# Hybrid diffusion step on one core: the last two column blocks of w_d go one token tile at a time, and three casts are issued sooner

## The chip, the core and the metric

The kernel runs on one core of one Trainium2 chip. The metric is the time of one execution on the device, in microseconds (us). Before the change three runs gave 1954.19, 1956.51 and 1957.05; the median is 1956.51. One further execution was profiled: it took 1956.43, and its span, from the first to the last instruction, is 1954.6. All views of the profile come from that one, and positions in it are given in us from the start of the span.

## The reference, cut to what matters

There are 384 tokens (128 of a context, 256 of a latent) of 2048 channels, in float32, and one layer. The change touches the dense SwiGLU feed-forward at the layer's end and the sums around it:

```python
h = rmsnorm(x, lw['norm_pre_ffn']) * (1.0 + sc2) + sh2
ff = (jax.nn.silu(h @ lw['w_ffn_gate']) * (h @ lw['w_ffn_up'])) @ lw['w_ffn_down']
x = x + ga2 * rmsnorm(ff, lw['norm_post_ffn'])
```

`w_ffn_gate` and `w_ffn_up` are 2048 x 5632, `w_ffn_down` is 5632 x 2048. The last line needs the whole of a token's row of `ff` before its root mean square is known. The output is the new `x`.

## The kernel before, in words

All products are made from float32 values cut into a high and a low part (`whi`, `wlo` for a weight, `hid_hi`, `hid_lo` for an activation); a product is three TensorE products, high by high, high by low, low by high. ScalarE casts the high part of each weight tile (L1430), VectorE subtracts for the low part (L1441), four of each are in store, and the two raw buffers are filled by DMAs that SyncE (SP) issues.

The 5632 hidden channels are worked through in 11 chunks of 512 (index `c`, `FC = 4` blocks of 128). For each chunk the gate and up products are made, the gated activation is turned so that hidden channels lie on partitions (`turn_hid`, L1596, into the PSUM tile `ptr`), cut into its two parts (L1598), and multiplied by the chunk's rows of `w_d` (`products`, L1532). The hand-written list `steps` sets the order of all of it; small pieces of work for ScalarE and VectorE are queued in the lists `now` and `pend`, and pieces of `pend` are taken out, three or so at a time, whenever the next weight is split (`split_next`, `settle_pend`). An engine runs its instructions in the order in which they were issued.

Partial sums of `ff` lie in twelve SBUF tiles `unit(t, n)` of 128 x 512, tile name `psums`: token tile `t` of 0 to 2, column block `n` of 0 to 3. The last chunk's activation, `hidE`, meets the eight last weights of `w_d`: for each column block, in the order 0, 2, 1, 3 (`d_order`), two weights of half a chunk each (`kh` 0 and 1). Every weight serves all three token tiles, 18 products; after a block's second weight `add_last` (L1676, L1677) adds the PSUM tile `pdn` to `unit(t, n)` and squares and sums it on ScalarE into `ssq`.

Behind the last product the root mean square of each token tile is formed in `r3` (`factor`, L1804 and L1805, and `inverse`, L1808). `scale` (L1813 on ScalarE, L1815 on VectorE) multiplies the units of token tiles 0 and 1, or, for tile 2, the identity `dg` (L1842). `turn(k, t)` turns a 128 x 128 piece into the PSUM tile `py[k]` (L1826, L1828), which holds all 384 tokens of 128 channels. Each `py[k]` is multiplied by the gate in `mods` and added to the residual `x1b`, by VectorE alone (L1862) or by ScalarE and GpSimd (L1855, L1856), and every second `k` a store of 384 KB goes to `out_yT` (L1867). Runs of 384 tokens of one channel are contiguous there.

`hid_sums` (L1606) forms sums of the activation for four products in place of more in the `w_d` part of chunks before the last; it is called from chunk 1 on a VectorE sum (`spare`, L1781), and from later chunks on the PSUM tiles.

Of the kernel before, what the change touches and what calls it, by code (L numbers as in the profile page):

```python
# [20 lines left out]
P = 128  # L21
# [75 lines left out]
def tile_step(ctx: ExitStack, tc: tile.TileContext, a, o):  # L97
# [947 lines left out]
    with ExitStack() as s:  # L1045
# [239 lines left out]
        def unit(t, n):  # L1285

            return psums[n // 2][:, 3 * (n % 2) + t, :]
# [310 lines left out]
            pend.extend([lambda: ACT.copy(hi, pt), lambda: DVE.tensor_sub(lo, pt, hi.bitcast(F32))])  # L1598
            return pt

        def hid_sums(h1, h2):

            r, (hi, lo) = dt["raw"], dt["S"]
            add, sub = DVE.tensor_add, DVE.tensor_sub
            return [
                lambda: ACT.copy(r[:, 3], h2[:, 0:2]),  # L1606
                lambda: add(r[:, 0], r[:, 3], h2[:, 2:4]), lambda: sub(r[:, 1], r[:, 0], h1[:, 0:2]),
                lambda: sub(r[:, 2], h1[:, 2:4], r[:, 1]), lambda: sub(r[:, 3], h1[:, 0:2], r[:, 3]),
                lambda: ACT.copy(hi, r),
            ]  # L1610
# [58 lines left out]

        ssq = pf.tile([P, 3, 4], F32, name="ssq")  # L1670
        r3 = pf.tile([P, 3], F32, name="r3")
        dg = ep[0][:, 0:P]

        def add_last(t, n, p, done):

# [11 lines left out]
        d_bank, hid_pt = {}, []  # L1687
        for kind, c, i in steps:
            last_c = c == NFC - 1 and kind == "D"
            if last_c and hid_last is not None and x1b is None:  # L1690
                while pend:
                    pend.pop(0)()
                x1b = actp.tile([P, KT, T], F32, tag="A_hi", name="x1b")
                for q in range(4):
                    SP.dma_start(x1b[:, 4 * q : 4 * q + 4, :], x1_d[:, 4 * q : 4 * q + 4, :])
                ACT.activation(tmp1, eps_t, AF.Sqrt)
            if kind == "D":
                w = grab2()
                n, kh = i // 2, i % 2
# [10 lines left out]
                    (pd_tiles[t], [[x[:, 2 * kh + m, t * P : (t + 1) * P] for m in range(2)] for x in h], mov_d, kh == 0, kh == 1)  # L1710
                    for t in ts
                ]
                products(w, todo, by_tile=last_c and kh == 1)
                if kh == 1:
                    if not last_c:
                        for t in range(3):
                            if c < LAST - 1:
                                pend.append(lambda k=10 + 3 * (n - 2) + t, p=pd_tiles[t], c=c: to_sums(k, p, c))
                            else:
                                pend.append(lambda u=unit(t, n), p=pd_tiles[t]: out(u, p))  # L1720
                    else:
                        if done < 3:
                            for t in range(3):
                                pend.append(lambda t=t, n=n, p=pd_tiles[t], d=done: add_last(t, n, p, d))
                        if done == 1:
                            pend.append(lambda: DVE.tensor_add(r3, ssq[:, :, 0], ssq[:, :, 1]))
                        if done == 2:
                            pend.append(lambda: DVE.tensor_add(r3, r3, ssq[:, :, 2]))
                        done += 1
                if (c, i) == (NFC - 2, 6):  # L1730

                    while pend:
                        pend.pop(0)()
                    hid_last = tuple(actp.tile([P, FC, T], F32R, tag=t, name="hidE") for t in ("C_hi", "C_lo"))
                    for t in range(3):
                        turn_hid(hid_last, t, psm, "mm")
            elif kind[0] == "D":
                w = grab2()
                while pend:
# [10 lines left out]
            else:  # L1750
# [19 lines left out]
                if kind == "A" and i:  # L1770
# [7 lines left out]
                    if c < LAST and i == 2:  # L1778
                        if c == 1:
                            f = dt["full"]  # L1780
                            pend.append(lambda: DVE.tensor_add(f, hid[0][:, :, P:T].bitcast(F32), hid[1][:, :, P:T].bitcast(F32)))  # L1781
# [19 lines left out]
        n = d_order[-1]  # L1801

        def factor(t):
            DVE.tensor_add(r3[:, t : t + 1], r3[:, t : t + 1], ssq[:, t, 3:4])  # L1804
            ACT.activation(r3[:, t : t + 1], r3[:, t : t + 1], AF.Sqrt, bias=eps_t[:, 0:1], scale=1.0 / D)  # L1805

        def inverse(t):
            DVE.reciprocal(r3[:, t : t + 1], r3[:, t : t + 1])  # L1808

        def scale(eng, t, n):  # L1810
            f = unit(t, n)
            if eng is ACT:
                ACT.mul(f, f, r3[:, t : t + 1])  # L1813
            else:
                eng.tensor_scalar_mul(f, f, r3[:, t : t + 1])  # L1815

        py = {}
        places = [(pss, "side")] * 5 + [(psm, "mm")] * 3

        def turn(k, t):  # L1820
            if k not in py:
                pool, tag = places[k % 8]
                py[k] = pool.tile([P, T], F32, tag=tag, name="py")
            dst, src = py[k][:, t * P : (t + 1) * P], unit(t, k // 4)[:, (k % 4) * P : (k % 4 + 1) * P]
            if t < 2:
                PE.transpose(dst, src, ident)  # L1826
            else:
                PE.matmul(dst, src, dg, start=True, stop=True)  # L1828

        add_last(0, n, pd_tiles[0], 3)  # L1830
        add_last(1, n, pd_tiles[1], 3)
        factor(0)
        factor(1)
        add_last(2, n, pd_tiles[2], 3)
        inverse(0)
        inverse(1)
        scale(DVE, 0, 0)
        scale(DVE, 1, 0)
        factor(2)
        scale(DVE, 0, 1)  # L1840
        inverse(2)
        DVE.tensor_scalar_mul(dg, ident, r3[:, 2:3])  # L1842
        scale(DVE, 1, 1)
        for k0, t in ((0, 0), (0, 1), (4, 0), (0, 2), (4, 1), (4, 2)):
            for k in range(k0, k0 + 4):
                turn(k, t)
        on_act = (1, 3, 5, 7, 9, 11)
        for k in range(KT):
            if k >= 8:
                for t in range(3):  # L1850
                    turn(k, t)
            if k in on_act:
                tmp = ep[1 + k // 2 % 5][:, 0:T]
                for lo, hi, cd in segs:
                    ACT.mul(tmp[:, lo:hi], py[k][:, lo:hi], mods[:, 5, k, cd : cd + 1])  # L1855
                POOL.tensor_add(x1b[:, k, :], x1b[:, k, :], tmp)  # L1856
                if k in (3, 7):
                    for t in range(2):
                        scale(ACT, t, 2 + k // 4)
            else:  # L1860
                for lo, hi, cd in segs:
                    DVE.scalar_tensor_tensor(  # L1862
                        x1b[:, k, lo:hi], py[k][:, lo:hi], mods[:, 5, k, cd : cd + 1], x1b[:, k, lo:hi],
                        op0=ALU.mult, op1=ALU.add,
                    )
            if k % 2:
                (ACT if k == KT - 1 else SP).dma_start(o["yT"][:, k - 1 : k + 1, :], x1b[:, k - 1 : k + 1, :])  # L1867


# [76 lines left out]
```

## Time and profile before

| what | value |
|---|---|
| median of three runs | 1956.51 us |
| the profiled execution's own time | 1956.43 us |
| its span | 1954.6 us |
| TensorE busy | 1935.7 us, 99% |
| VectorE busy | 1639.9 us, 84% |
| ScalarE busy | 1011.9 us, 52% |
| GpSimd busy | 144.4 us, 7% |
| last product of w_d issued | 1937.6 us |
| last addition to the residual ends | 1949.9 us |

A group in the profile is written as line, engine, operation, output tile <- input tiles, shape. PE is TensorE, DVE VectorE, ACT ScalarE, POOL GpSimd, SPq the queue of SyncE that issues DMAs. What stands in square brackets is how long the engine was idle just before and whose end released it. Modelled ends of TensorE products overlap, so two starts in a row say more than one duration.

### The profile page before, as it was taken

The page shows a single profiled execution, that of the slowest core. Times are in us where ns is not written, and L with a number is a line of the kernel's source. Part 1 is how long each engine was busy: PE and PEld are TensorE (multiplying, and loading weights), DVE is VectorE, ACT ScalarE, POOL GpSimd, SP SyncE. Part 2 cuts the span into 40 slices and gives each one's busy share as a digit, 9 for nine tenths or more (in the row PEclk, how much of TensorE's full clock was granted, in tenths as well). Part 3 has the DMA queues.
Part 4 walks back from the last instruction along what each step waited for, and adds up shares of the span by engine and source line. Part 5 has one row for each costly group of instructions (what it writes and reads, how often), then busy time and mean ns, then how long its engine had stood idle before and what let it go on. Part 6 is the DMA issues. An engine that isn't in the chain of part 4 may idle for free.

```text
span 1954.6 us, 28091 instructions
## 1 busy us (share of the span) xinstructions
PE 1935.7 (99%) x10522; PEld 1715.2 (88%) x10522; DVE 1639.9 (84%) x2047; ACT 1011.9 (52%) x1468; POOL 144.4 (7%) x172
## 2 busy tenths in 40 slices
PE   8999999999999999999999999999999999999998
PEld 6779999999999999999988888888888888888876
DVE  5569788878876797977799989999999999988975
ACT  4233454454335655446456555555556565656444
POOL 0000000000000000004000111111112021111001
PEclk9999999999999999999999999999999999999999
DMA  9977677767764687655447686786869595949463
GB/s 389 374 259 266 222 251 238 226 220 258 249 200 155 218 269 242 215 173 201 144 145 245 160 237 171 217 206 194 222 182 234 169 239 158 264 117 254 134 212 108
DMA packets 212456, 422.05 MB, mean 216 GB/s; under 512 B 16732, under 2 KB 115228, under 8 KB 207968
## 3 DMA queue, kind: packets, MB, share of 16 engines
q1 hardware_dynamic: 193744, 386.31, 58.8%
q0 software_dynamic: 18432, 33.56, 11.1%
q8 instruction: 82, 1.34, 0.3%
q14 instruction: 54, 0.44, 0.1%
q10 hardware_dynamic: 144, 0.39, 0.1%
HBM read 365.68 MB, written 54.53 MB: 215 GB/s over the span
## 4 chain that ended last, share of the span: by engine, by line
PE 94%; DMA 2%; DVE 2%; ACT 1%; issue 0%; SPq 0%; POOL 0%; DVEq 0%; ACTq 0%; POOLq 0%
PE pmm L258 35%; PE pgu L1532 30%; PE pdn L1532 10%; PE pds L1532 7%; PE pv L398 3%; PE pgm L381 1%; DMA slab<-in_w_ada 1%; PE pf L996 1%; PE px L416 1%; PE pmm L1251 1%; PE ptr L1596 1%; DMA raw<-in_w_d 1%; DVE wlo L1441 1%; PE po L645 1%; PE pf L997 0%
## 5 line engine op out<-in xcount | busy, mean ns | idle before, releaser
L258 PE MATMUL pmm<-A_hi,whi 128*128 128x384 f32 x1200 | 404.5, 337 | 0.0
L258 PE MATMUL pmm<-A_hi,wlo 128*128 128x384 f32 x1200 | 401.6, 335 | 0.0
L258 PE MATMUL pmm<-A_lo,whi 128*128 128x384 f32 x1200 | 401.5, 335 | 0.0
L1430 ACT CAST whi<-u 128x1024 fp32r<-128x1024 f32 x200 | 209.5, 1052 | 154.2 <-PE pgu L1532 49.9
L224 ACT CAST whi<-raw 128x1024 fp32r<-128x1024 f32 x181 | 190.0, 1052 | 187.7 <-DMA raw<-in_w_gate 65.7
L225 DVE TENSOR_TENSOR wlo<-raw,whi 128x1024 fp32r<-128x1024 f32 x179 | 218.4, 1222 | 57.0 <-ACT whi L224 56.2
L1430 ACT CAST whi<-raw 128x1024 fp32r<-128x1024 f32 x157 | 165.4, 1053 | 185.0 <-DMA raw<-in_w_d 49.4
L1441 DVE TENSOR_TENSOR wlo<-u,whi 128x1024 fp32r<-128x1024 f32 x200 | 242.6, 1220 | 17.3 <-ACT whi L1430 16.6
L1532 PE MATMUL pgu<-whi,A_hi 128*128 128x512 f32 x640 | 252.5, 394 | 1.4 <-ACT ep L1573 0.9
L1532 PE MATMUL pgu<-whi,A_lo 128*128 128x512 f32 x640 | 249.6, 390 | 0.0
L258 PEld LDWEIGHTS pmm<-A_hi,whi 128*128 128x128 f32 x1200 | 225.4, 188 | 2.9 <-issue 1.8
L258 PEld LDWEIGHTS pmm<-A_lo,whi 128*128 128x128 f32 x1200 | 225.4, 188 | 0.2
L258 PEld LDWEIGHTS pmm<-A_hi,wlo 128*128 128x128 f32 x1200 | 225.3, 188 | 0.0
L572 DVE SCALAR_TENSOR_TENSOR adacc<-adaw,spad,adacc 128x1024 f32<-128x1024 f32 x180 | 222.9, 1280 | 2.5 <-DMA adaw<-in_w_ada 2.3
L1441 DVE TENSOR_TENSOR wlo<-raw,whi 128x1024 fp32r<-128x1024 f32 x157 | 191.6, 1220 | 15.3 <-ACT whi L1430 12.9
L1532 PE MATMUL pgu<-wlo,A_hi 128*128 128x512 f32 x640 | 186.0, 390 | 0.0
L1532 PEld LDWEIGHTS pgu<-whi,A_hi 128*128 128x128 f32 x640 | 120.2, 188 | 28.9 <-ACT whi L1430 2.0
L1532 PEld LDWEIGHTS pgu<-wlo,A_hi 128*128 128x128 f32 x640 | 120.2, 188 | 25.5
L1532 PEld LDWEIGHTS pgu<-whi,A_lo 128*128 128x128 f32 x640 | 120.3, 188 | 24.2
L1532 PE MATMUL pgu<-whi,S 128*128 128x512 f32 x400 | 117.6, 392 | 0.0
L1642 POOL DMA_DIRECT2D sums_d<-dw x64 | 58.4, 948 | 642.5 <-ACT dw L1638 637.2
L1532 PE MATMUL pdn<-whi,hid_hi 128*128 128x512 f32 x264 | 102.8, 390 | 0.0
(401 smaller groups left out, 3273.0 us busy)
## 6 DMA issues: line engine op xcount, KB each, us to landing
adaw<-in_w_ada SPq DMA_DIRECT2D x96, 512.0 KB, 4.3
raw<-in_w_d SPq DMA_DIRECT2D x70, 512.0 KB, 3.7
slab<-in_w_ada SPq DMA_DIRECT2D x32, 1024.0 KB
raw<-in_w_gate SPq DMA_DIRECT2D x64, 512.0 KB, 4.5
raw<-in_w_g SPq DMA_DIRECT2D x48, 512.0 KB, 4.7
raw<-in_w_u SPq DMA_DIRECT2D x48, 512.0 KB, 6.3
raw<-in_w_in SPq DMA_DIRECT2D x44, 512.0 KB, 4.5
u<-in_w_u SPq DMA_DIRECT2D x40, 512.0 KB, 7.6
```

Source lines behind the costliest of these rows:

```text
L224: ACT.copy(hi, raw)
L225: sub = lambda: eng.tensor_sub(lo, raw, hi.bitcast(F32))
L258: PE.matmul(dst, w[wi][:, k * n + n0 : k * n + n0 + P], x[xi][:, k0 + k, :], start=first and k == 0 and j == 0, stop=last and k == kts - 1 ...
L381: PE.matmul(pgv[q : q + 32, :], spad[:, k, :], slab[k // (KT // 2)][:, k % (KT // 2), :], start=k < 4, stop=k >= KT - 4,)
L398: PE.matmul(pv[2 * t + g], hT[x_][:, kb, t * P : (t + 1) * P], w_[:, g * 512 : (g + 1) * 512], start=kb == 0 and j == 0, stop=kb == KT - 1 ...
L416: PE.matmul(px, w_[:, u * P : (u + 1) * P], hT[x_][:, kb, :], start=j == 0, stop=j == 2)
L572: DVE.scalar_tensor_tensor(acc[:, c, :], w, spad[:, k, c : c + 1], acc[:, c, :], op0=ALU.mult, op1=ALU.add,)
L645: PE.matmul(dst, w[wi], x[xi], start=first and j == 0, stop=last and j == 2)
L1430: ACT.copy(hi, src)
L1441: DVE.tensor_sub(lo, src, hi.bitcast(F32))
L1532: PE.matmul(dst, stat[x_][m], mov(w[w_], m), start=first and w_ == m == x_ == 0, stop=last and w_ == m == 1, skip_group_check=any(more),)
L1642: POOL.dma_start(sums_d[k], u, accum_op=ALU.add)
```

## The change

Four things are changed.

First, in `hid_sums` for chunk 1 the copy of L1606 is issued on VectorE and no longer on ScalarE.

Second, after the last activation is turned (`turn_hid` for `hidE`), its three casts and then its three low parts are issued at once; before they stayed in `pend` behind the next weight's cast.

Third, the last two column blocks (`n` 1 and 3, four weights) are no longer run weight by weight. The four weights are collected in `late_w`, and `block(t, g)` runs the six products of weight `g` for one token tile `t` only. So tile 0 goes through all four weights, then tile 1, then tile 2.

Fourth, the tail is by token tile. When tile `t` has its last sum, `factor` forms its root mean square and scales all its four units, two on VectorE and two on ScalarE. Its 16 pieces are turned in groups of four into one PSUM tile (`bk`, eight banks, planned by hand in `sums_at` and `turned_at`), between the blocks of the next tile. `residual` adds 128 x 128 pieces on VectorE, or multiplies four on ScalarE and adds them at once on GpSimd. `store` sends four channel blocks of one token tile: 256 KB, in runs of 512 bytes, twelve stores on SP in place of eight.

```diff
-        def hid_sums(h1, h2):
+        def hid_sums(h1, h2, copy=ACT.copy):
...
-                lambda: ACT.copy(r[:, 3], h2[:, 0:2]),
+                lambda: copy(r[:, 3], h2[:, 0:2]),
...
+            if last_c and done >= 2:
+                late_w.append(grab2())
+                if len(late_w) == 4:
+                    while pend:
+                        pend.pop(0)()
+                continue
...
-                products(w, todo, by_tile=last_c and kh == 1)
+                products(w, todo)
...
                     for t in range(3):
                         turn_hid(hid_last, t, psm, "mm")
+                    for x in (0, 2, 4, 1, 3, 5):
+                        pend[x]()
+                    pend.clear()
...
-                            pend.extend(hid_sums(f[:, :, 0:P], f[:, :, P:]))
+                            pend.extend(hid_sums(f[:, :, 0:P], f[:, :, P:], DVE.tensor_copy))
...
+        bk = [pss.tile([P, 512], F32, tag="side", name="bk") for _ in range(5)]
+        bk += [psm.tile([P, 512], F32, tag="mm", name="bk") for _ in range(3)]
+        sums_at = ((5, 3), (6, 4), (7, 0))
+        turned_at = ((1, 2, 5, 3), (6, 4, 1, 2), (5, 3, 7, 0))
+
+        def block(t, g, fill=()):
+            n, kh = d_order[2 + g // 2], g % 2
+            stat = [[x[:, 2 * kh + m, t * P : (t + 1) * P] for m in range(2)] for x in hid_last]
+            products(late_w[g], [(bk[sums_at[t][g // 2]], stat, mov_d, kh == 0, kh == 1)])
+            if kh:
+                add_last(t, n, bk[sums_at[t][g // 2]], 2 + g // 2)
+                if fill:
+                    turn(1, 1)
+                    for _ in range(2):
+                        fill.pop(0)()
+                r = r3[:, t : t + 1]
+                DVE.tensor_add(r, r, ssq[:, t, 2 + g // 2 : 3 + g // 2])
+
+        def factor(t, fill=()):
+            r = r3[:, t : t + 1]
+            if fill:
+                fill.pop(0)()
+            ACT.activation(r, r, AF.Sqrt, bias=eps_t[:, 0:1], scale=1.0 / D)
+            DVE.reciprocal(r, r)
+            for n in (0, 2, 1, 3):
+                f = unit(t, n)
+                if n < 2:
+                    DVE.tensor_scalar_mul(f, f, r)
+                else:
+                    ACT.mul(f, f, r)
+            if fill:
+                fill.pop(0)()
+
+        def turn(t, n):
+            for j in range(4):
+                dst, src = (x[:, j * P : (j + 1) * P] for x in (bk[turned_at[t][n]], unit(t, n)))
                 PE.transpose(dst, src, ident)
...
+        def residual(t, n, on_act=False, later=False):
+            p = bk[turned_at[t][n]].rearrange("p (j c) -> p j c", j=4)
+            x = x1b[:, 4 * n : 4 * n + 4, t * P : (t + 1) * P]
+            g = lambda j: mods[:, 5, 4 * n + j, min(t, 1) : min(t, 1) + 1]
+            tmp = ep[4 + n % 2].rearrange("p (j c) -> p j c", j=4)
+            def add(j):
+                DVE.scalar_tensor_tensor(x[:, j, :], p[:, j, :], g(j), x[:, j, :], op0=ALU.mult, op1=ALU.add)
+
+            if later:
+                return [lambda j=j: add(j) for j in range(4)]
+            for j in range(4):
+                if on_act:
+                    ACT.mul(tmp[:, j, :], p[:, j, :], g(j))
+                else:
+                    add(j)
+            if on_act:
+                POOL.tensor_add(x, x, tmp)
+
+        def store(t, n):
+            SP.dma_start(o["yT"][:, 4 * n : 4 * n + 4, t * P : (t + 1) * P], x1b[:, 4 * n : 4 * n + 4, t * P : (t + 1) * P])
+
+        for g in range(4):
+            block(0, g)
         factor(0)
...
+        for t in (1, 2):
+            block(t, 0)
+            block(t, 1)
+            turn(t - 1, 0)
+            turn(t - 1, 2)
+            block(t, 2)
+            if t == 1:
+                turn(0, 1)
+            turn(t - 1, 3)
+            residual(t - 1, 0)
+            residual(t - 1, 2, True)
+            if t == 1:
+                residual(0, 1)
+            residual(t - 1, 3, True)
+            fill = []
+            if t == 2:
+                fill = residual(1, 1, later=True)
+            block(t, 3, fill)
+            factor(t, fill)
+            for n in (0, 2, 3, 1):
+                store(t - 1, n)
+        for n in (0, 2, 1, 3):
+            turn(2, n)
+            residual(2, n, n == 2)
+        for n in (0, 1, 2, 3):
+            store(2, n)
```

On VectorE, at the sums of chunk 1 (`dw` is the tile of the sums, `spare` the whole activation, `u` and `raw` weights):

```order
 L1413 TENSOR_TENSOR u_9223<-u_9221,u_9223 128x1024
 L1441 TENSOR_TENSOR wlo<-u_9222,whi 128x1024
-L1781 TENSOR_TENSOR spare<-hid_hi,hid_lo 128x1024
+L1786 TENSOR_TENSOR spare<-hid_hi,hid_lo 128x1024
+L1606 COPY dw<-spare 128x256
 L1607 TENSOR_TENSOR dw<-dw,spare 128x256
 L1441 TENSOR_TENSOR wlo<-raw,whi 128x1024
```

The copy now stands between the sum it reads and the addition that reads it, on the same engine; on ScalarE it stood ahead of two evictions of L1573.

On ScalarE, at the last activation and the last weights of `w_d`:

```order
-L1430 CAST whi<-raw 128x1024 x6
+L1430 CAST whi<-raw 128x1024 x5
 L1598 CAST hidE<-ptr 128x4x128 x3
-L1696 ACT_TABLE_LOAD
-L1696 ACTIVATE tmp_88<-eps_t 128x1
+L1430 CAST whi<-raw 128x1024
+L1695 ACT_TABLE_LOAD
+L1695 ACTIVATE tmp_88<-eps_t 128x1
 L1430 CAST whi<-raw 128x1024 x3
```

The three casts of `hidE` moved ahead of one weight cast.

On TensorE, the end of the program before (`py` the turned output, `ep_7617` the scaled identity):

```order
-L1532 MATMUL pdn<-whi,hidE 128x512 x4
-L1532 MATMUL pdn<-wlo,hidE 128x512 x2
-L1826 MATMUL py<-ident,psums 128x128 x12
-L1828 MATMUL py<-ep_7617,psums 128x128 x4
-L1826 MATMUL py<-ident,psums 128x128 x4
```

and a stretch of it now, from the second block of the second token tile:

```order
+L1532 MATMUL bk<-whi,hidE 128x512 x4
+L1532 MATMUL bk<-wlo,hidE 128x512 x2
+L1842 MATMUL bk<-ident,psums 128x128 x8
+L1532 MATMUL bk<-whi,hidE 128x512 x4
+L1532 MATMUL bk<-wlo,hidE 128x512 x2
+L1842 MATMUL bk<-ident,psums 128x128 x8
```

All turns stood behind the last product; now 28 of 48 stand between the blocks of the second and third token tile, and 4 more behind the last product and ahead of the third tile's own.

More of the change, by code (lines that the diff above doesn't have):

```diff
@@ L1686, in tile_step @@
         pd_tiles, hid_last, x1b, done = None, None, None, 0
-        d_bank, hid_pt = {}, []
+        d_bank, hid_pt, late_w = {}, [], []
         for kind, c, i in steps:
@@ L1721, in tile_step @@
                     else:
-                        if done < 3:
-                            for t in range(3):
-                                pend.append(lambda t=t, n=n, p=pd_tiles[t], d=done: add_last(t, n, p, d))
+                        for t in range(3):
+                            pend.append(lambda t=t, n=n, p=pd_tiles[t], d=done: add_last(t, n, p, d))
                         if done == 1:
                             pend.append(lambda: DVE.tensor_add(r3, ssq[:, :, 0], ssq[:, :, 1]))
-                        if done == 2:
-                            pend.append(lambda: DVE.tensor_add(r3, r3, ssq[:, :, 2]))
                         done += 1
@@ L1800, in tile_step @@
             pend.pop(0)()
[L1801 to L1830, printed above, removed]
@@ L1831, in tile_step @@
-        add_last(1, n, pd_tiles[1], 3)
-        factor(0)
[L1833 to L1867, printed above, removed]
+        bk = [pss.tile([P, 512], F32, tag="side", name="bk") for _ in range(5)]
```

1 line of the change is left out of this document (removed).

## Prediction

> **What bounds the kernel now.** I read the page's chain first, then the table of what TensorE waited for, then the three places of that table in time. The chain that ended last, by engine:
>
> ```profile
> PE 94%; DMA 2%; DVE 2%; ACT 1%; issue 0%; SPq 0%; POOL 0%; DVEq 0%; ACTq 0%; POOLq 0%
> ```
>
> So time comes off only where TensorE waits, or behind its last product. The waits of TensorE (us in total, times, longest) that the change touches:
>
> ```profile
> PE pdn L1532 <- DVE hidE L1598: 1.9, 2, 1.4
> PE py L1826 <- DVE psums L1815: 1.6, 1, 1.6
> PE pgu L1532 <- ACT ep L1573: 0.9, 1, 0.9
> ```
>
> Place one, the third row, in the timeline (start, duration):
>
> ```profile
> 980.48 0.61 PE L1532 MATMUL pgu<-wlo,S 128*128 128x512 f32 x2
> 982.04 0.50 PE L1532 MATMUL pgu<-whi,A_hi 128*128 128x512 f32 x1 [0.94 <-ACT ep L1573]
> ...
> 977.60 1.04 ACT L1430 CAST whi<-raw 128x1024 fp32r<-128x1024 f32 x1
> 981.10 0.40 ACT L1606 COPY dw<-spare 128x256 f32<-128x256 f32 x1 [2.46 <-DVE spare L1781]
> 981.41 1.07 ACT L1573 COPY ep<-pgu 128x512 f32<-128x512 f32 x2
> ...
> 979.85 1.22 DVE L1781 TENSOR_TENSOR spare<-hid_hi,hid_lo 128x1024 f32<-128x1024 f32 x1
> 981.54 0.43 DVE L1607 TENSOR_TENSOR dw<-dw,spare 128x256 f32<-128x256 f32 x1 [0.47 <-ACT dw L1606]
> ```
>
> ScalarE stands 2.46 us behind VectorE's sum for the small copy of L1606, and the two evictions that TensorE needs are queued behind it.
>
> Place two, the last inner activation, and the start of the second and the fifth of the last eight w_d weights:
>
> ```profile
> 1896.98 1.51 PE L1596 MATMUL ptr<-ident,ep 128*128 128x128 f32 x12
> 1901.09 1.52 PE L1532 MATMUL pdn<-wlo,hid_hi 128*128 128x512 f32 x6
> 1904.00 1.19 PE L1532 MATMUL pdn<-whi,hidE 128*128 128x512 f32 x4 [1.39 <-DVE hidE L1598]
> 1909.05 1.07 PE L1532 MATMUL pdn<-whi,hidE 128*128 128x512 f32 x4
> 1921.29 2.88 PE L1532 MATMUL pdn<-whi,hidE 128*128 128x512 f32 x12
> 1929.45 2.88 PE L1532 MATMUL pdn<-whi,hidE 128*128 128x512 f32 x12
> ...
> 1898.83 1.05 ACT L1430 CAST whi<-raw 128x1024 fp32r<-128x1024 f32 x1 [4.10 <-DMA raw<-in_w_d]
> 1901.69 1.05 ACT L1430 CAST whi<-raw 128x1024 fp32r<-128x1024 f32 x1 [1.81 <-DMA raw<-in_w_d]
> 1902.65 1.55 ACT L1598 CAST hidE<-ptr 128x512 fp32r<-128x512 f32 x3
> ...
> 1899.91 1.23 DVE L1441 TENSOR_TENSOR wlo<-raw,whi 128x1024 fp32r<-128x1024 f32 x1 [2.13 <-ACT whi L1430]
> 1905.00 1.28 DVE L1598 TENSOR_TENSOR hidE<-ptr,hidE 128x512 fp32r<-128x512 f32 x2
> ```
>
> The turned blocks are in PSUM at 1898.5, but ScalarE first waits until 1901.69 for a weight's DMA and casts that.
>
> Place three is the tail behind the fifth weight, from Z = 1921.29 to the span's end, 1954.6: 33.3 us.
>
> **The change, part by part.** Every term is in the clock of the profiled execution (span 1954.6, its own time 1956.43, which is 0.08 under the median, 1956.51).
>
> *The copy of L1606 to VectorE.* The two products at 980.48 are issued 0.227 apart (1921.29 to 1929.45 holds 36: 8.16/36), so the next was due at 980.93 and came at 982.04: 1.1 us lost. Without the copy in front, the evictions follow the cast that ends at 978.64, so TensorE no longer waits. VectorE takes the copy into the 0.47 us that it idled before L1607; no row shows a VectorE copy of 128x256, and ScalarE's 0.40 and the 0.43 of L1607 bound it: nothing to 0.1 us, off TensorE's path. If VectorE's later splits run short of that, the price is the whole 1.1. **-1.1**, between -1.1 and 0.
>
> *The three casts, issued at the turn.* They go in front of one weight cast, the one at 1901.69, and stay behind the one at 1898.83. ScalarE is free at 1899.88 and casts until 1901.4; VectorE, free from its split at 1901.1, makes the three low parts at 0.6 each: 1901.8, 1902.4, 1903.0. The first weight may start where its predecessor's products end, 1901.09 + 6 x 0.227 = 1902.45, and then reaches the second and third token tile after four products (0.9 us) each, at 1903.4 and 1904.3, both behind their low parts. Before, the weight ended at 1909.05, and 1902.45 + 18 x 0.227 is 1906.53: **-2.5**. The weight cast that is put behind follows at 1901.69 at worst, where its DMA held it before, and its weight is wanted only two weights (8.2 us) after 1902.45. SP's loads wait for the splits as before, so none is later. If the DMA of the weight cast at 1898.83 came later, all of this would move with it.
>
> *The tail.* A token tile now takes the last four weights in a row, 24 products, 24 x 0.227 = 5.44 us; the three tiles have 72, as before: 16.3 us from Z. Rows for the chain behind a tile's last product, here of the second tile of before:
>
> ```profile
> 1936.25 1.07 PE L1532 MATMUL pdn<-whi,hidE 128*128 128x512 f32 x4
> 1936.45 0.69 DVE L1676 TENSOR_TENSOR psums<-psums,pdn 128x512 f32<-128x512 f32 x1 [0.67 <-PE pdn L1532]
> 1937.98 0.16 DVE L1804 TENSOR_TENSOR r<-r,ssq 128x1 f32<-128x1 f32 x1 [0.78 <-ACT ep L1677]
> 1939.84 0.29 ACT L1805 ACTIVATE r<-r,eps_t 128x1 f32<-128x1 f32 x1 [0.28 <-DVE r L1804]
> 1940.16 0.17 DVE L1808 RECIPROCAL r<-r 128x1 f32<-128x1 f32 x1
> 1939.39 1.53 PE L1826 MATMUL py<-ident,psums 128*128 128x128 f32 x12 [1.63 <-DVE psums L1815]
> ...
> L1815 DVE TENSOR_SCALAR psums<-psums,r 128x512 f32<-128x512 f32 x4 | 1.8, 481 | 0.0
> L1862 DVE SCALAR_TENSOR_TENSOR x1b<-py,mods,x1b 128x256 f32<-128x256 f32 x10 | 4.8, 476 | 0.0
> L1862 DVE SCALAR_TENSOR_TENSOR x1b<-py,mods,x1b 128x128 f32<-128x128 f32 x10 | 3.5, 347 | 1.9 <-PE py L1828 1.8
> L1856 POOL TENSOR_TENSOR x1b<-x1b,ep 128x384 f32<-128x384 f32 x6 | 5.9, 994 | 133.9 <-ACT ep L1855 133.9
> ...
> 1947.19 2.69 DVE L1862 SCALAR_TENSOR_TENSOR x1b<-py,mods,x1b 128x128 f32<-128x128 f32 x8 [0.84 <-PE py L1828]
> ```
>
> The tile's products end where the next begin, 1936.25; its sum of r begins 1.73 us later. Then 0.16, square root 0.04 + 0.29, reciprocal 0.03 + 0.17, scaling 0.04 + 0.48, and 0.06 to the first turn: 3.0 us. Two blocks of products of the next tile (2.72) lie beside it, so TensorE waits 0.28 for each of the first two tiles: 0.6. Turns add to TensorE 28 times the pitch of 0.105 (12 from 1896.98, next product 1.26 later) before the third tile's last block: 2.9. So its products end at Z + 19.8, its chain at Z + 22.8, four turns later (0.7 with their latency) VectorE starts 12 additions of 128x128. Eight of both sizes take 2.69, which with 0.347 and 0.476 makes a pitch near 0.26: 11 x 0.26 + 0.35 = 3.2, the last ending at Z + 26.7 against 1949.9 = Z + 28.6 before. Beside it run four multiplications on ScalarE (taken like VectorE's additions, 1.1) and POOL's addition of 512 columns (994 ns for 384, so 1.3): from the second turn on, Z + 23.9, they end at Z + 26.3, within the additions. The pieces of the first two tiles lie beside products.
>
> The stores are not hidden. Before, by stretches of 1 us (DMA share and GB/s last), then slices of 0.1 us from 1943.0, the issue of the first store, and what the write packets cost beside those of two loads:
>
> ```profile
> 1952.00:1953.00 1.00, 0.00 (x0) 0.00 (x0) 0.00 (x0) 0.00 (x0) 0.00 (x0) 0.75 1.03 393
> 1953.00:1954.00 1.00, 0.00 (x0) 0.00 (x0) 0.00 (x0) 0.00 (x0) 0.00 (x0) 0.50 0.08 28
> ...
> DMA  0000000000009999799996999997999610006988
> ...
> 1943.35 6.70 SPq L1867 DMA_DIRECT2D out_yT<-x1b  x7
> ...
> q10 hardware_dynamic: 144, 0.39, 5.2%
> ...
> q1 hardware_dynamic: 334, 0.34, 33.0%
> ...
> q1 hardware_dynamic: 272, 0.52, 12.4%
> ```
>
> Data ends near 1953.1, 1.5 us before the span does, and starts 0.85 after the issue at 1943.35. A store of before has 3 KB packets: 128 of them and 16 short ones take 5.2% of 16 engines over 20 us, 0.13 us a packet. The change's stores have runs of 512 B, which no row shows. A load of 1 KB packets (334, 33.0% over 3.5 us) takes 55 ns each, one of 2 KB (272, 12.4% over 12 us) 88. Half the bytes cost well over half the time; the line through both gives 121 at 3 KB, where the stores stand, and 39 at 512 B. I take 39: the two nearest rows make it, and it holds for writes as far as the trace shows them. Its bounds: 21 (a sixth of the 3 KB packet) and 55. A store of 512 packets over 16 engines then takes 32 x 39 = 1.25 us. The third tile's first store can go after four additions, Z + 24.5; its data begins 0.9 later; four stores: 25.4 + 5.0, and the 1.5: Z + 31.9. Before it was Z + 33.3: **-1.4**. That TensorE's product phase ends 3.4 us later than before (Z + 19.8 against Z + 16.4) is paid from what no longer stands behind it.
>
> *Covers that must hold.* The eighth weight is wanted by the first tile already at Z + 4.1, not Z + 12.2. Its split now queues behind three additions that start together (0.2 + 1.9) and ends at Z + 3.3; its low part is wanted at Z + 5.0. Cover 1.7; each us beyond costs one. SP issues the twelve stores alone; nothing is behind them.
>
> Sum: -1.1 - 2.5 - 1.4 = -5.0, 1956.43 - 5.0 = **1951.4**.
>
> **The rivals.** *Stores at line rate.* At 21 ns a store takes 0.67 and the last additions set the end: Z + 26.7 + 0.9 + 0.7 + 1.5 = Z + 29.8, -3.5 there, -7.1 in all: 1949.3. For it: the 3 KB packets of 0.13 us; against: 55 and 88 do not stand as one to two. The Trainium skill (DMA: Bandwidth & Descriptors, Specifications) puts line rate at 512 B and above, which is this rival; the two load rows speak against it.
>
> *Stores at the 1 KB price*, 55 ns: 1.76 each. The first tile's first store can go near Z + 11.5 (six blocks, the wait, a sum that waits for the second tile's square, four additions), and then the queue hardly empties: 11.5 + 0.9 + 12 x 1.76 + 0.4 + 1.5 = Z + 35.4, +2.1, in all -1.5: 1954.9.
>
> *Slower: short packets make the store queue the bound.* If a packet costs by its number, 88 ns as the 2 KB one, a store takes 2.8: 11.5 + 0.9 + 33.8 + 1.5 = Z + 47.7, +14.4, in all +10.8: 1967.2. It passes no change from 60 ns and +0.2% from 71. For it: 6144 packets in place of 1024; against: packets of 1 KB at 55.
>
> *The scaling chain isn't covered.* If ScalarE is in a piece of four multiplications when a tile's square or root asks, some 1.1 us (4 x 0.26, as VectorE's) comes on the chain for each of the first two tiles: +2.2, 1953.6. For it: ScalarE has eight such pieces queued ahead of each last square; against: my times let it finish 0.9 earlier.
>
> **How the numbers follow.** What a measurement can tell from no change is about 0.2%, 3.9 us: below 1952.6 is faster. Forecast 0.52 and line rate 0.15: faster 0.67. The 1 KB price 0.13 and the uncovered chain 0.10: same 0.23. Short packets: slower 0.10. The range runs from the line-rate case to the 1 KB price, 1949.3 to 1954.9, and 0.3 wider at each end for the gap between one execution and a median: 1949.0 to 1955.2. Only the slower case lies outside.
>
> **What the profile after would show.** Right: no wait for L1573 near 981; none or under 0.3 us for hidE, and the first weight's products at 1901 to 1902; two short waits (0.2 to 0.5) for scaling between the last blocks; the last addition 5 to 6 us earlier than 1949.9; store packets near 40 ns. Wrong: a DMA share near full from the first tile's stores on; a TensorE wait on whi or wlo of the eighth weight; TensorE waits elsewhere that eat the 1.1 or the 2.5.

## The result and the profile after

After the change the median of 20 runs is 1952.29 us (1950.11 to 1954.63); 20 runs of the kernel before beside them gave 1956.59 (1954.19 to 1959.02). The ratio after to before is 0.998, with a 95% interval of 0.9973 to 0.9986: 4.3 us faster, just over the 0.2% that a measurement of this kernel can tell. The profiled execution took 1951.26 with a span of 1949.5, 5.1 less than the span of before. The forecast was 1951.4, 0.9 under the median.

The chain that ended last, from the page of after, is as full of TensorE as before:

```profile
PE 95%; DVE 2%; DMA 1%; ACT 1%; issue 0%; SPq 0%; POOL 0%; DVEq 0%; ACTq 0%; POOLq 0%
```

Place one in the timeline of after:

```profile
980.23 1.22 DVE L1786 TENSOR_TENSOR spare<-hid_hi,hid_lo 128x1024 f32<-128x1024 f32 x1
...
980.88 0.62 PE L1532 MATMUL pgu<-wlo,S 128*128 128x512 f32 x2
...
981.33 0.39 PE L1532 MATMUL pgu<-whi,A_hi 128*128 128x512 f32 x1
...
981.49 0.29 DVE L1606 COPY dw<-spare 128x256 f32<-128x256 f32 x1
...
981.81 0.43 DVE L1607 TENSOR_TENSOR dw<-dw,spare 128x256 f32<-128x256 f32 x1
```

The products that follow the two on `wlo,S` start 0.45 behind them and wait for nobody; before it was 1.56. The copy takes 0.29 on VectorE, in what was idle time.

Place two, the last inner activation:

```profile
1898.39 1.05 ACT L1430 CAST whi<-raw 128x1024 fp32r<-128x1024 f32 x1 [5.22 <-DMA raw<-in_w_d]
...
1899.34 1.56 ACT L1598 CAST hidE<-ptr 128x512 fp32r<-128x512 f32 x3
...
1900.30 1.52 PE L1532 MATMUL pdn<-wlo,hid_hi 128*128 128x512 f32 x6
1900.62 1.88 DVE L1598 TENSOR_TENSOR hidE<-ptr,hidE 128x512 fp32r<-128x512 f32 x3
...
1901.66 2.88 PE L1532 MATMUL pdn<-whi,hidE 128*128 128x512 f32 x12
...
1905.74 0.61 PE L1532 MATMUL pdn<-whi,hidE 128*128 128x512 f32 x2
```

The casts run straight behind the one weight cast, the three low parts end at 1902.5, and no product waits. From the six products on `wlo,hid_hi` to the second weight of `hidE` it is 5.44 us now (1905.74 less 1900.30), and was 7.96.

The tail starts at Z = 1917.98 and takes 31.5 us. The two short waits of TensorE, the chain of the third token tile and its turns and additions:

```profile
1925.69 0.61 PE L1532 MATMUL bk<-wlo,hidE 128*128 128x512 f32 x2
...
1926.42 1.09 PE L1842 MATMUL bk<-ident,psums 128*128 128x128 f32 x8
...
1933.26 0.61 PE L1532 MATMUL bk<-wlo,hidE 128*128 128x512 f32 x2
...
1933.99 1.09 PE L1842 MATMUL bk<-ident,psums 128*128 128x128 f32 x8
...
1936.67 1.18 PE L1532 MATMUL bk<-whi,hidE 128*128 128x512 f32 x4
...
1937.68 0.62 PE L1532 MATMUL bk<-wlo,hidE 128*128 128x512 f32 x2
...
1938.34 0.69 DVE L1675 TENSOR_TENSOR psums<-psums,bk 128x512 f32<-128x512 f32 x1 [1.42 <-PE bk L1532]
...
1941.14 1.97 PE L1842 MATMUL bk<-ident,psums 128*128 128x128 f32 x16 [2.40 <-DVE psums L1833]
1941.39 3.63 DVE L1850 SCALAR_TENSOR_TENSOR x1b<-bk,mods,x1b 128x128 f32<-128x128 f32 x13
```

Two products at a pitch of 0.227 were over at 1926.14 and 1933.71, so each turn came 0.28 late. Behind the last product and four turns TensorE is idle for 2.40 us, which becomes important below. The last addition ends at 1945.02, Z + 27.04, but the end comes 4.48 later, behind stores. Stretches of 1 us (columns: length, busy time of the five engines, clock, DMA share, GB/s):

```profile
1945.00:1946.00 1.00, 0.00 (x0) 0.00 (x0) 0.03 (x1) 0.00 (x0) 0.00 (x0) 1.00 0.99 284
1946.00:1947.00 1.00, 0.00 (x0) 0.00 (x0) 0.00 (x0) 0.00 (x0) 0.00 (x0) 1.00 0.99 286
1947.00:1948.00 1.00, 0.00 (x0) 0.00 (x0) 0.00 (x0) 0.00 (x0) 0.00 (x0) 0.52 0.70 209
```

The DMA engines are full, at 286 GB/s, where the 3 KB packets of before reached 393. In packets of 512 B this is 16 x 0.99 / 559 a us = 28.4 ns each.

The balance between the two profiled executions, in us from one common place of the program to the next:

| stretch | before | after | difference |
|---|---|---|---|
| start to the products on `wlo,S` (nothing changed here) | 980.48 | 980.88 | +0.40 |
| these to the next product | 1.56 | 0.45 | -1.11 |
| to the turns of the last activation (nothing changed here) | 914.94 | 914.89 | -0.05 |
| six products on `wlo,hid_hi` to the second last weight | 7.96 | 5.44 | -2.52 |
| Z to the end | 33.31 | 31.52 | -1.79 |

Between these rows lie only products and turns, so that makes -5.07, the difference of the spans (-5.1) to within what the rows round. The third row is alike by chance; copy_on_act, below, shows why. Spans are printed to 0.1 us, so a tail is good to 0.05.

### The profile page after: what moved, and what is told of

It reads as the page before. It is cut to its first block, busy times and chain, and to the rows that moved or that the text cites. A ratio compares the mean times of both kernels' runs of the same rounds, so it can differ in the third digit from the quotient of the medians.

```text
span 1949.5 us, 28077 instructions
## 1 busy us (share of the span) xinstructions
PE 1932.7 (99%) x10506; PEld 1712.5 (88%) x10506; DVE 1641.2 (84%) x2059; ACT 1015.1 (52%) x1477; POOL 145.2 (7%) x171
## 4 chain that ended last, share of the span: by engine, by line
PE 95%; DVE 2%; DMA 1%; ACT 1%; issue 0%; SPq 0%; POOL 0%; DVEq 0%; ACTq 0%; POOLq 0%
PE pmm L258 35%; PE pgu L1532 30%; PE pdn L1532 10%; PE pds L1532 7%; PE pv L398 3%; PE pgm L381 1%; PE pf L996 1%; DMA slab<-in_w_ada 1%; PE px L416 1%; PE pmm L1251 1%; PE ptr L1596 1%; PE pf L997 1%; PE bk L1532 1%; PE po L645 1%; DVE wlo L1441 0%
## 5 line engine op out<-in xcount | busy, mean ns | idle before, releaser
L1532 PEld LDWEIGHTS pgu<-whi,A_hi 128*128 128x128 f32 x640 | 120.1, 188 | 26.7 <-issue 1.2
```

The lines of the kernel that those rows point to most:

```text
L1532: PE.matmul(dst, stat[x_][m], mov(w[w_], m), start=first and w_ == m == x_ == 0, stop=last and w_ == m == 1, skip_group_check=any(more),)
```

## The experiments

The theory: three separate gains, -1.1 at place one, -2.5 at place two, -1.4 to -1.8 in the tail, the last set by what a short packet costs. Rivals: the weights' splits on VectorE, or other work there, take back what place one gives; the tail is bound by additions, not stores; a packet costs by its number.

**One part undone at a time.** Copy back on ScalarE:

```diff
-pend.extend(hid_sums(f[:, :, 0:P], f[:, :, P:], DVE.tensor_copy))
+pend.extend(hid_sums(f[:, :, 0:P], f[:, :, P:]))
```

> The changed kernel with the copy of L1606 for chunk 1 back on ScalarE; nothing else differs. Theory (the three gains stand one behind the other on TensorE's queue): the products after the two low-part products near 981 start 1.5 to 1.6 us after them instead of 0.45, and the whole 1.1 arrives at the end: the span is 1950.6 instead of 1949.5, and the distance from the fifth w_d weight's first product to the end stays 31.5. Rival (VectorE's splits are the true limit behind 981, so TensorE's 1.1 is taken back before the end): the wait is there, but the span stays within 0.3 of 1949.5.

The wait is back, by the same releaser and of the same size, in the timeline of this kernel:

```profile
981.64 0.40 ACT L1606 COPY dw<-spare 128x256 f32<-128x256 f32 x1 [2.46 <-DVE spare L1786]
...
982.58 0.50 PE L1532 MATMUL pgu<-whi,A_hi 128*128 128x512 f32 x1 [0.94 <-ACT ep L1573]
```

Place one costs 1.56 again, the tail 31.52. Its median was 1953.16, ratio to before 0.9979 (0.997 to 0.9988), which does not tell it from the changed kernel. The 1.1 us are shown where they arise, not at the end: the unchanged stretch from there to the last turns, 914.89 in after, took 914.12 here and 914.5 to 918.0 in the other kernels whose copy is on VectorE.

Part of the gain is lost again in that stretch. The same group of products in the page of copy_on_act and, below it, in that of after (count, busy time, mean, then the idle time before them and who ended it):

```profile
L1532 PE MATMUL pdn<-whi,hid_hi 128*128 128x512 f32 x264 | 102.8, 389 | 0.0
...
L1532 PE MATMUL pdn<-whi,hid_hi 128*128 128x512 f32 x264 | 102.9, 390 | 0.2 <-DVE hid_lo L1598 0.2
```

The wait is one product, 99 us behind place one. In after TensorE could have started it at 1079.85, but VectorE finished a low part of the next activation (`hid_lo`, L1598) only at 1080.20, and the product started at 1080.26, 0.41 late. In before TensorE came to this product at 1080.65, and the low part had been ready since 1079.90. All eleven profiles with the copy on VectorE have this gap, 0.17 to 0.85 beyond the pitch (0.5 in the mean); before, copy_on_act and copy_x17, with the copy on ScalarE, have none. So in after some 0.7 of the 1.11 is left behind this point. That the stretch took as long in before (914.94) is chance: before lost 0.61 there to a weight, at 1136.6, which after did not. The copy did not make the low part late: counted from the two products on `wlo,S`, it ends 99.32 on in after, 99.43 in before and 99.28 in copy_on_act. It stayed where it was, while TensorE is due there at 98.97 in place of 100.17.

Casts left in `pend`:

```diff
-for x in (0, 2, 4, 1, 3, 5):
-    pend[x]()
-pend.clear()
```

> The changed kernel with the three casts of the last activation and their low parts back in the pending list, behind the next weight's cast; the new tail stays. Theory: from the last six products with hid_hi to the second of the last eight weights it takes 7.9 us again instead of 5.4, and the span is 1952.0 (2.5 more); the distance from the fifth weight to the end stays 31.5. Rival (the new tail needs the late weights so early that the 2.5 is hidden behind a wait for the seventh or eighth weight): the span is under 1951.

```profile
1899.29 1.52 PE L1532 MATMUL pdn<-wlo,hid_hi 128*128 128x512 f32 x6
1899.57 1.05 ACT L1430 CAST whi<-raw 128x1024 fp32r<-128x1024 f32 x1 [0.79 <-DMA raw<-in_w_d]
...
1900.52 1.55 ACT L1598 CAST hidE<-ptr 128x512 fp32r<-128x512 f32 x3
...
1901.88 1.20 PE L1532 MATMUL pdn<-whi,hidE 128*128 128x512 f32 x4 [1.07 <-DVE hidE L1598]
...
1903.62 0.73 PE L1532 MATMUL pdn<-whi,hidE 128*128 128x512 f32 x2 [0.54 <-DVE hidE L1598]
```

In its timeline the weight cast stands in front of the three casts again, and TensorE waits for `hidE` again: place two takes 7.63, against 7.96 before and 5.44 after (the weight's DMA landed some 0.3 sooner than in before). 1954.28; ratio 0.9992 (0.9983 to 1.0). Place two is the largest of the three. The tail was 32.24 and not the 31.5 expected: the clock fell in it too (last section).

The old tail, that is, the kernel before with only the two edits above made:

> The kernel before with the copy of L1606 on VectorE and the three casts issued at the turn, and its own tail by column blocks and 3 KB store packets. Theory: 1.1 and 2.5 less than before, span 1951.0, and the distance from the fifth weight to the end is 33.3, so that the new tail alone is worth 1.5 to 1.8. Rival (the tail is worth nothing by itself, the store queue ends both alike): span 1949.5 to 1950.0.

Z to the end is 33.31, as it was before; places one and two are as in after. So the tail alone is worth 1.8. The profiled execution was the slowest of this kernel's eleven (1957.47; span 1955.6), because its stretch between places one and two took 917.99; the median is 1953.36, ratio 0.9986 (0.9977 to 0.9995).

**Is the 1.1 carried to the end?** Seventeen copies on ScalarE in place of one:

```diff
-lambda: copy(r[:, 3], h2[:, 0:2]),
+lambda: [copy(r[:, 3], h2[:, 0:2]) for _ in range(17 if f1 else 1)],
...
-pend.extend(hid_sums(f[:, :, 0:P], f[:, :, P:], DVE.tensor_copy))
+pend.extend(hid_sums(f[:, :, 0:P], f[:, :, P:], f1=True))
```

> The changed kernel with the copy of L1606 for chunk 1 on ScalarE again and issued 17 times in a row; the 16 further copies write the same values and are work that is only added. A copy follows another after 0.31 us there, so the evictions behind them come 5.0 us later. Theory (what TensorE loses at 981 arrives at the end): the start-to-start gap there is 1.56 + 5.0 = 6.6 us, the distance from the product after it to the turns of the last activation stays at 914 to 915.5 as in the other profiles, and the time is some 6 us above the changed kernel's 1952.3, near 1958. Rival (the weights' splits, not TensorE, set the pace behind 981): the gap is 6.6, but that distance shrinks to 911 or less and the time stays under 1955.

```profile
980.79 7.38 ACT L1606 COPY dw<-spare 128x256 f32<-128x256 f32 x17 [2.46 <-DVE spare L1786]
...
988.70 0.79 PE L1532 MATMUL pgu<-whi,A_hi 128*128 128x512 f32 x1 [7.92 <-ACT ep L1573]
```

The copies follow each other every 0.436 us, more than I took, so the gap is 8.53: 7.0 more than with one copy. The span is 1958.2, 8.0 over copy_on_act's. 1961.76; ratio 1.0024 (1.0014 to 1.0033). A wait of this length reaches the end, against the rival. It cost even more, since the granted clock fell behind it; two stretches of this kernel:

```profile
987.00:989.00 2.00, 0.30 (x1) 0.30 (x2) 0.80 (x2) 1.94 (x5) 0.00 (x0) 0.50 0.00 0
989.00:1066.00 77.00, 77.00 (x331) 63.51 (x331) 71.67 (x74) 45.06 (x54) 0.00 (x0) 0.97 0.65 211
```

To the next turns of an activation TensorE took 86.67 us here and 84.46 in copy_on_act, so the clock cost 2.2. Without them the stretch behind place one, 915.91, is 913.7, 0.4 below copy_on_act's: hardly anything came back.

A wait as short as 1.1 is not passed on whole: see the gap at 1080 above. How much of it arrives at the end stays open: the unchanged stretch varies by more than that from execution to execution, with waits of 0.2 to 0.9, for weights too, that jump about in it.

**What a packet costs.** The output laid out so that a store's four channel blocks of one token tile are one run of 2 KB in memory:

```diff
-SP.dma_start(o["yT"][:, 4 * n : 4 * n + 4, t * P : (t + 1) * P], x1b[...])
+SP.dma_start(o["yT"][:, t, 4 * n : 4 * n + 4, :], x1b[...])
```

> The changed kernel with its output laid out so that each store writes 2 KB of one partition in one run, 128 packets in place of 512; the same bytes and the same twelve stores, and the output is put in order on the host by another transposition. Theory (the last stores are held by the price of 512-byte packets, 29 ns each in the profile after, 0.92 us a store): a store takes about 0.7 us, the queue no longer holds the last one, and the span is 0.7 to 1.0 shorter, 1948.6; the distance from the fifth weight to the end is 30.6. Rival (the end is the last addition plus a fixed latency of the last store): the distance stays 31.5 within 0.2.

```profile
1947.00:1948.00 1.00, 0.00 (x0) 0.00 (x0) 0.00 (x0) 0.00 (x0) 0.00 (x0) 1.00 0.99 272
...
DMA packets 2321, 1.16 MB, mean 193 GB/s; under 512 B 64, under 2 KB 2321, under 8 KB 2321
```

The edit did not do what I meant: by this stretch of its end the DMA engines are full at 272 GB/s, as in after, and the last addition is again 4.48 ahead of the end (tail 31.64). The packets, counted in the second line from 1942 to 1948, stayed at 512 B: that is the length of the runs in `x1b`, and they are cut by it although memory has runs of 2 KB. 1951.35; ratio 0.9973 (0.9964 to 0.9983). It stands as a repetition of the changed kernel, and against it copy_on_act, measured beside it, is 1.8 slower by the medians, casts_late 2.9 and old_tail 2.0; each ratio's interval is near 2 us to either side, so only casts_late is set apart.

The additions then wrote to a tile with the same 2 KB runs:

```diff
+yo = actp.tile([P, 3, KT, P], F32, tag="A_lo", name="yo")
-DVE.scalar_tensor_tensor(x[:, j, :], p[:, j, :], g(j), x[:, j, :], ...)
+DVE.scalar_tensor_tensor(y[:, j, :], p[:, j, :], g(j), x[:, j, :], ...)
-SP.dma_start(..., x1b[...])
+SP.dma_start(..., yo[:, t, 4 * n : 4 * n + 4, :])
```

> As long_runs, and the sums are written to an SBUF tile of their own that is laid out by token tile, so that a store reads and writes 2 KB of a partition in one run on both sides. Theory (packets are cut where either side's run ends, and the last stores are held by their price): the packets of the twelve stores are of 2 KB, a store takes about 0.7 us instead of 0.92, and the distance from the fifth w_d weight's first product to the end falls from 31.5 to 30.6 or 30.8. Rival (the end is the last addition plus a fixed latency): it stays within 0.2 of 31.5.

Windows and timeline of this kernel:

```profile
1942.00:1943.00 1.00, 1.00 (x7) 1.00 (x6) 0.45 (x2) 0.39 (x1) 0.00 (x0) 0.50 0.00 0
...
1947.00:1948.00 1.00, 0.00 (x0) 0.00 (x0) 0.00 (x0) 0.00 (x0) 0.00 (x0) 1.00 1.04 389
...
DMA packets 611, 1.12 MB, mean 187 GB/s; under 512 B 64, under 2 KB 64, under 8 KB 611
```

```profile
1941.60 3.61 PE L1843 MATMUL bk<-ident,psums 128*128 128x128 f32 x16 [2.40 <-DVE psums L1834]
```

Now packets have 2 KB and 389 GB/s, and the end is 3.69 behind the last addition in place of 4.48: by this 0.8 of the tail was the short packets (0.6 in long_busy, below, where the clock holds). But this execution's tail is 31.87, no better, because behind the 2.40 us wait the clock stood at 0.50: sixteen turns took 3.61 in place of 1.97, and the last addition ended at Z + 28.18. 1951.45; ratio 0.997 (0.9958 to 0.9981).

To go the other way, I cut each store's runs to 256 B. A first try only rearranged the view of the same store and left packets and DMAs as they were:

> The changed kernel with each store cut in two of 64 tokens: runs of 256 B, 24 stores, the same bytes. Theory (a packet costs a fixed part and a part by its bytes: 29 ns at 512 B after the change and 126 at 3 KB before give 39 ns a KB and 9 fixed, so 19 at 256 B): the third tile's data takes 4.9 us instead of 3.7, and the distance from the fifth weight to the end is 32.7. Rival (short runs cost more than in proportion, the mechanism of the case in which the change would have been slower): the store queue never empties from the first tile on, and the distance is over 36. The Trainium skill (DMA: Bandwidth & Descriptors, Specifications) says that a transfer under 512 B is read, modified and written back; that would be this rival.

It says nothing on packets; one run, 1952.53, tail 31.53. Two stores of 64 tokens each do it:

```diff
-SP.dma_start(o["yT"][..., t * P : (t + 1) * P], x1b[...])
+for h in range(2):
+    at = slice(t * P + 64 * h, t * P + 64 * h + 64)
+    SP.dma_start(o["yT"][:, 4 * n : 4 * n + 4, at], x1b[:, 4 * n : 4 * n + 4, at])
```

> The changed kernel with each store issued as two of 64 tokens, 24 stores with runs of 256 B (in runs_256 the view alone was rearranged and the stores stayed as they were). Theory (a fixed part and a part by bytes; 29 ns at 512 B, 87 at 2 KB give 19 fixed... 9 to 10 and 39 a KB, so 19 at 256 B): the third tile's data takes 4.9 us instead of 3.7, and the distance from the fifth weight to the end is 32.7. Rival (short runs cost more than in proportion): the store queue does not empty from the first tile on, and the distance is over 36.

```profile
1943.00:1944.00 1.00, 1.00 (x7) 1.00 (x6) 0.62 (x3) 0.02 (x1) 0.00 (x0) 0.50 0.21 49
...
1947.60:1948.60 1.00, 0.00 (x0) 0.00 (x0) 0.00 (x0) 0.00 (x0) 0.00 (x0) 1.00 0.97 218
```

The second stretch has 16 x 0.97 / 852 a us = 18.2 ns a packet of 256 B, where the theory had 19. One run, 1954.04; the tail is 33.23, against the rival's 36 and more. 1.1 of it is again the clock at 0.50 behind the wait (the first stretch; last addition Z + 28.18), and the end lies 5.05 behind that addition.

**The waits of TensorE in the tail.** The third block of the next tile put ahead of the first turns:

```diff
+            block(t, 2)
             turn(t - 1, 0)
             turn(t - 1, 2)
-            block(t, 2)
```

> The changed kernel with the first eight turns of each finished token tile behind the third block of the next tile instead of the second. Theory (TensorE waits 0.28 for the scaling of each of the first two tiles, and all that follows hangs on it): both waits go, the third tile's last product comes 0.55 earlier after the fifth weight, and the distance from there to the end falls from 31.5 to 31.0. Rival (ScalarE's eight multiplications, then 0.8 later, reach into the third tile's last square): the product comes earlier, but the first turn of the third tile does not, and the distance stays 31.5.

In the timeline the turns stand straight behind products, at a pitch of 0.45 for the two before them:

```profile
1927.35 0.62 PE L1532 MATMUL bk<-wlo,hidE 128*128 128x512 f32 x2
1927.80 1.91 PE L1842 MATMUL bk<-ident,psums 128*128 128x128 f32 x16
...
1941.02 1.97 PE L1842 MATMUL bk<-ident,psums 128*128 128x128 f32 x16 [2.67 <-DVE psums L1833]
```

Both waits are gone and the tail is 31.02, 0.5 shorter. The third tile's last product comes 0.7 earlier after Z, but the wait ahead of its turns has grown from 2.40 to 2.67. 1951.57; ratio 0.9972 (0.9961 to 0.9984): by the time alone it cannot be told from after.

Long packets, and ten products whose results nobody uses in the 2.40 us wait:

```diff
+for k in range(10):
+    PE.matmul(bk[5], hid_last[0][:, k % 4, 2 * P : T], mov_d(late_w[3][0], 0), start=True, stop=True)
```

> As long_both, and TensorE makes ten products of 512 columns that nothing uses (into a bank that is free there) while it waits for the third tile's scaling; that work is only added. Theory (in long_both the granted clock fell to half in that wait and made the last turns and additions 1.1 us longer; the 2 KB packets themselves gave what was expected): the clock stays at 1.0 through the last turns, the last addition ends 27.0 after the fifth weight's first product, as in the changed kernel, the end comes 3.7 behind it instead of 4.5, and the distance from the fifth weight to the end is 30.7. Rival (the long stores cost as much as the short ones, and the clock had no part): the distance is 31.5 or more.

```profile
1937.51 2.56 PE L1892 MATMUL bk<-whi,hidE 128*128 128x512 f32 x10
...
1940.15 1.97 PE L1843 MATMUL bk<-ident,psums 128*128 128x128 f32 x16
```

The turns take 1.97, the last addition ends at Z + 27.04 and the program 3.86 later: the tail is 30.90, the shortest measured, 0.6 under after's. 1950.91; ratio 0.9976 (0.9966 to 0.9986). Beside it on the same chip the changed kernel was run again:

> The changed kernel once more, for a comparison with all_busy on the same chip and for a second profile of it. Theory: the gap near 981 is 0.45, from the last six products with hid_hi to the second of the last eight weights it takes 5.4 us, from the fifth weight to the end 31.5 (32.2 if the clock falls to half in the third tile's wait); the span itself varies by some 1.5 us with waits elsewhere. Rival (the profile after was a lucky one): the three distances differ by over 0.5 from these.

1951.49; ratio 0.9976 (0.9967 to 0.9985), the same as long_busy's. The start-to-start gap near 981 (0.46) and place two (5.46) are as expected. In this execution too the clock fell to 0.50 behind the wait, and the tail is 32.41.

Last, both together, with the third tile's scaling moved into the identity of its turns:

```diff
+if t == 2:
+    DVE.tensor_scalar_mul(dg, ident, r)
-    PE.transpose(dst, src, ident)
+    PE.matmul(dst, src, dg, start=True, stop=True)
```

> As long_busy, with the first turns behind the third block as in turns_later, and for the third token tile the scaled identity in place of four scaled units, as the kernel before did it. Theory (the parts add): 30.7 less 0.5 for the two waits and 0.2 for the shorter scaling, 30.0 from the fifth weight to the end against 31.5; its time is some 1.5 below the changed kernel's. Rival (ScalarE's later multiplications and the third tile's turns, which now hang on one scaling each, fill the gap): not under 30.6.

```profile
1941.59 3.84 PE L1850 MATMUL bk<-ep,psums 128*128 128x128 f32 x32 [0.21 <-DVE ep L1834]
1942.79 1.13 DVE L1859 SCALAR_TENSOR_TENSOR yo<-bk,mods,x1b 128x128 f32<-128x128 f32 x4 [0.99 <-PE bk L1850]
```

A miss: a product with a scaled identity is two instructions where a turn is one (32 for 16 pieces), and takes 3.84 in place of 1.97. The additions waited 0.99 and 0.66 for it, and the tail is 31.39. 1951.84; ratio 0.9981 (0.9973 to 0.999). The two gains without this scaling were not run.

## Why the prediction was right

**Place one, -1.1:** -1.11 where it arises; the wait goes, and the copy costs 0.29 (forecast 0.1 or nothing) under cover. But the term had a price if VectorE's later work fell short, which the sum set at nothing, and it was paid in part: 0.41 went again at 1080, where TensorE, now earlier, waits for VectorE's `hid_lo`. That the total came near the forecast all the same is in part luck: before lost 0.61 further on, at 1136.6, and after did not, and the tail gave 0.4 more than forecast. **Place two, -2.5:** -2.52, with the three low parts ahead of the products that want them. **The two waits for the scaling**, 0.28 each: 0.28 each. **The third tile's chain**, 3.0: from where its products ended, 1938.14 by their pitch, to the first turn, 1941.14, is 3.0.

**The tail, -1.4:** -1.79, with three small misses that partly cancel. Its products end at Z + 20.2 (forecast Z + 19.8), because the four products behind each group of turns take 1.01 (1936.67 to 1937.68) and not four pitches, 0.91, so all behind them is 0.3 to 0.4 late: the last addition at Z + 27.04 (Z + 26.7), the data of the third tile's first store near Z + 25.8 (Z + 25.4). The mis-sized term is the packet of 512 B: 39 ns from a straight line through two loads, 28.4 measured. A store then takes 32 x 0.0284 = 0.91 in place of 1.25, and four of them 3.9 with the gaps (5.0). From the last data, near 1947.7, to the end it is 1.75 (1.5). 25.8 + 3.9 + 1.75 = 31.5 against 31.9. The stores now stand on a line of their own: 18.2 ns at 256 B, 28.4 at 512, 88 at 2 KB (16 x 1.04 / 190 a us), and the 0.13 us at 3 KB of before. It gives 48 at 1 KB, so the load's 55 was the dearer row, and drawing the line through it made 39.

**The rivals.** Line rate: the end would have been Z + 29.8, with 0.67 a store; 286 GB/s beside 389 at 2 KB rule it out. The Trainium skill (DMA: Bandwidth & Descriptors, Specifications) puts line rate at 512 B and above; the measurement disagrees. The same place gives a read-modify-write below 512 B; packets of 256 B at 18.2 ns show no such price in these writes. The 1 KB price is ruled out by 28.4 against 55; packets that cost by their number by 18.2, 28.4 and 88, which grow with the bytes. The uncovered scaling chain did not come: nothing stood ahead of it on ScalarE.

The median fell by 4.3 where the profiles differ by 5.1; the profiled execution of after is the fifth fastest of the twenty. The clock's drop in the new tail, next, may be part of that; it is not shown.

## What to carry to other kernels

Split a change into the places where the bound engine waits, and price each by distances between fixed points of the program that lie near each other: here the three agree between executions to 0.2 us or better while the clock holds, where whole times differ by 4 us. When a wait is gone, look behind it for one that was not there before: the engine comes earlier, and those it waits for may not. When work at the end is cut finer so that it overlaps, price its stores by the length of their packets, and remember that short runs on the SBUF side cut them even where memory has long ones. Where TensorE idles just before a short last burst, look at its granted clock, not only at the wait.

## What the hardware showed that I had not expected

With the new tail TensorE idles for 2.40 us behind its last product and four turns (2.67 in turns_later). In four of the ten profiles that have this wait (after_again, casts_late, long_both, runs_256b) the granted clock fell to 0.50 for the turns behind it and the last addition came 0.8 to 1.1 later; in the other six it did not. Two stretches of after_again, the turns among them:

```profile
1941.50:1942.50 1.00, 1.00 (x6) 1.00 (x7) 0.69 (x3) 0.77 (x2) 0.00 (x0) 0.64 0.22 61
1942.50:1943.50 1.00, 1.00 (x7) 1.00 (x6) 1.00 (x4) 0.20 (x1) 0.00 (x0) 0.50 0.46 134
```

With ten products in the wait it stayed at 1.0 in both profiles that have them (long_busy, all_busy); as it held in six of ten without them, two do not show that the products did it. The Trainium skill (TensorE: Matmul & The Clock Gate, Part 1: The HAM clock gate) has the clock at half after an idle window of about 3.4 us that runs freely, and so depends on where the window falls. A drop in some executions and not in others fits that; but the 2.40 us of idle time that were enough here are shorter than the page's figure.
